# The mixer's last projection as seven block products, with weight sums made in DRAM and ten modulation sums moved

## The chip, the core and the metric

The kernel runs on one core of a Trainium2 chip, in one launch. The metric is the device time of that core in microseconds (us). TensorE multiplies, VectorE (DVE) and ScalarE (ACT) do elementwise work, GpSimd (POOL) does elementwise work and issues DMAs, and SyncE (SP) issues DMAs.

## What is computed

One block with 1024 positions and 1024 channels, all float32:

```python
h = rms_norm(x, norm_mix_g) * (1 + sc1) + sh1
proj = h @ w_in                                  # 7168 columns
y_a = (b * causal_dwconv3(c * v)) @ w_short_out
u = causal_dwconv31(v2 * sigmoid(gl)) + bias
y_b = silu(layer_norm(u)) @ w_conf_out
mix = (g_a * y_a + g_b * y_b) @ w_o              # the projection that changes
x = x + g1 * mix
h2 = rms_norm(x, norm_ffn_g) * (1 + sc2) + sh2
a, bgate = split(h2 @ w_ffn_in, 2)
x = x + g2 * ((silu(a) * bgate) @ w_ffn_out)
out = rms_norm(x, final_norm_g)
```

`sh1, sc1, g1, sh2, sc2, g2` are six modulation vectors, `silu(c) @ w_ada + b_ada`, of 1024 each.

## The kernel before

Activations lie transposed, 128 channels on the partitions and the 1024 positions in two halves `h` of 512 columns. Every operand is held as a high part `h` in fp32r and a remainder `l`, and a product of a 128x128 weight block with a 128x512 operand is three matmuls, high by high, low by high and high by low (`mm3`, L505, L506, L508). Weights come by `load` (SP, L228) into the `raw` buffers, ScalarE casts the high part `wh` (L244), and VectorE or GpSimd subtracts to get `wl` (L245). `fetch` keeps `AHEAD` = 2 weights in front of the one in use.

Most projections run in duals: two output blocks of 128 rows at a time, as a Strassen-like scheme with seven products, `"1265734"` (`PRODUCTS`). `product` is one of them: 2 x 4 x 3 = 24 matmuls of 512 columns. "1" and "2" take plain weight blocks, "4" too, and "5", "6", "7" and "3" take sums of weight blocks, as well as sums of operand blocks. The stages on the profile are: the first norm (to 65 us), the projection of the inputs, 12 duals `w_duals` (65 to 561; from dual 3 on the remainders are GpSimd's), the short convolution's projection `ya` (to 635), the conformer's `yb` (to 711), the last one `mix` (to 799), the feed-forward part's first projection, 11 duals (to 1222), its second (to 1411), and the last norm.

In `mix`, alone among them, no seven products are used: `col_block` makes 8 blocks of output rows in each of the two halves, each from 8 weight blocks, 2 x 8 x 8 x 3 = 384 matmuls. Its evacuation (L1471, VectorE) is x + g1 times the result, with x reloaded as `xr` (GpSimd's queue, L1466); the new x goes to `x1_dram` (L1474) and its square (ScalarE, L1475) into one running sum per half (VectorE, L1481). The sum of the first half is taken over the partitions by TensorE inside `mix` (`norm_2_first`), the second's in the first product of the feed-forward part. Ten modulation sums (numbers 30 to 39 in `ADA_ORDER`) are made there too: `load_b` loads 512 KB from `ada`, and VectorE multiplies and adds in one instruction (`modulation_of`, L486).

The weight sums of `yb` are made in SBUF (`conf_units`): six accumulating DMAs on GpSimd's queue (L398) and two additions on VectorE. Gates `gb` are loaded on that queue too (L1431), and half of the merged results `ma` are summed there by accumulating DMAs (L1403). The first two duals of the feed-forward part make their weight sums by VectorE (`dual_units`). A wait of one engine's instruction holds all that stand behind it on that engine; a scheduler sets the order of each engine from the program and from `issue_after`, and TensorE's order may interleave two products.

## Time and profile before

| | us |
|---|---|
| median of 3 runs | 1442.96 (1442.72 to 1443.38) |
| the profiled execution | 1443.7 |
| its span | 1441.9 |
| TensorE busy | 1428.6 (99%), 6322 matmuls |
| VectorE busy | 1198.8 (83%) |
| ScalarE busy | 655.2 (45%) |
| GpSimd busy | 522.0 (36%) |

The granted clock was 0.998. A row of a group names the line, the engine, the operation and what it writes and reads (`out<-in`), then the shape and the count. A row of waits gives who waited for whom, us in total, how often, and the longest. A row of the table by stage gives the stretch in us from the span's start, its length, the busy time and instructions of each engine, TensorE's granted clock, the busy share of the 16 DMA engines (the sum of the packets' time, so it can pass 1) and the GB/s moved. A row of a DMA queue gives packets, MB and the share of 16 engines; a row of DMA issues the count, the KB of one, and the median us from issue to landing.

### The profile page before, as it was taken

Reading aid. Unit: us, or ns where it says so; the run is one execution under the profiler, and the core shown is the slowest. Engines: PE = TensorE matmul, PEld = TensorE weight load, DVE = VectorE, ACT = ScalarE, POOL = GpSimd, SP = SyncE. Lnnn points to the kernel's source line nnn. Section 1 sums busy time; section 2 is a strip of 40 time slices with the busy share of each in tenths; the row PEclk is TensorE's granted clock in tenths of the full one; section 3 lists DMA queues with packets and bytes.
Section 4 is the critical chain, followed back from the end, with each engine's and each line's share of the span. In section 5 each row is a group of like instructions: output and inputs, shape, how many; then the busy total and the mean of one; then the engine's idle time right before and its main releaser. Section 6 shows DMA issues by size and latency. Waiting matters only on the chain.

```text
span 1441.9 us, 17770 instructions
## 1 busy us (share of the span) xinstructions
PE 1428.6 (99%) x6322; PEld 1173.5 (81%) x6322; DVE 1198.8 (83%) x1665; ACT 655.2 (45%) x963; POOL 522.0 (36%) x512
## 2 busy tenths in 40 slices
PE   8999999999999999999999999999999999999997
PEld 4888888888888888888888888888888888888887
DVE  7996999999899999989988898877777665866676
ACT  4873333333343457567426474533444443321235
POOL 0017777777677562013311001110111015563405
PEclk9999999999999999999999999999999999999999
DMA  9743233333335578768886248645555449996903
GB/s 349 282 162 90 72 117 117 103 117 103 132 124 183 161 244 296 219 193 203 223 317 228 79 141 267 205 149 186 185 175 161 138 143 358 389 372 191 340 0 117
DMA packets 95946, 275.04 MB, mean 191 GB/s; under 512 B 10945, under 2 KB 12993, under 8 KB 95858
## 3 DMA queue, kind: packets, MB, share of 16 engines
q1 hardware_dynamic: 46672, 148.92, 30.6%
q0 software_dynamic: 44000, 111.36, 25.6%
q10 hardware_dynamic: 5186, 13.64, 2.5%
q8 instruction: 49, 0.80, 0.2%
q14 instruction: 39, 0.32, 0.1%
HBM read 203.09 MB, written 67.63 MB: 188 GB/s over the span
## 4 chain that ended last, share of the span: by engine, by line
PE 97%; POOL 1%; DVE 0%; issue 0%; POOLq 0%
PE bank L506 14%; PE bank L505 14%; PE bank L508 14%; PE x L508 8%; PE x L506 8%; PE x L505 8%; PE z L506 4%; PE z L508 4%; PE z L505 4%; PE y L508 3%; PE y L506 3%; PE y L505 3%; PE mix L506 2%; PE mix L508 2%; PE mix L505 2%; PE lead L501 1%
## 5 line engine op out<-in xcount | busy, mean ns | idle before, releaser
L244 ACT CAST wh<-raw 128x1024 fp32r<-128x1024 f32 (+2 forms) x254 | 263.0, 1037 | 394.7 <-PE bank L506 138.1
L245 DVE TENSOR_TENSOR wl<-raw,wh 128x1024 fp32r<-128x1024 f32 (+2 forms) x176 | 212.4, 1208 | 38.1 <-ACT wh L244 35.5
L245 POOL TENSOR_TENSOR wl<-raw,wh 128x1024 fp32r<-128x1024 f32 x78 | 194.4, 2500 | 91.1 <-ACT wh L244 90.1
L1168 DVE SCALAR_TENSOR_TENSOR c<-diff,vec,c 128x512 f32<-128x512 f32 x232 | 163.4, 749 | 1.5
L1644 POOL DMA_DIRECT2D hid<-stage x70 | 37.4, 535 | 343.3 <-DVE stage L554 326.8
L505 PE MATMUL bank<-th,wh 128*128 128x512 f32 x336 | 130.7, 389 | 0.0
L506 PE MATMUL bank<-tl,wh 128*128 128x512 f32 x336 | 130.7, 389 | 0.0
L508 PE MATMUL bank<-th,wl 128*128 128x512 f32 x336 | 130.7, 389 | 0.0
L505 PEld LDWEIGHTS bank<-th,wh 128*128 128x128 f32 x336 | 63.1, 188 | 13.2
L508 PEld LDWEIGHTS bank<-th,wl 128*128 128x128 f32 x336 | 63.1, 188 | 13.1
L506 PEld LDWEIGHTS bank<-tl,wh 128*128 128x128 f32 x336 | 63.1, 188 | 13.0
L553 ACT CAST stage<-g 128x512 fp32r<-128x512 f32 x60 | 37.3, 622 | 74.7 <-DMA hid<-stage 41.0
L506 PE MATMUL x<-tl,wh 128*128 128x512 f32 x176 | 68.5, 389 | 0.0
L505 PE MATMUL x<-th,wh 128*128 128x512 f32 x176 | 68.5, 389 | 0.0
L508 PE MATMUL x<-th,wl 128*128 128x512 f32 x176 | 68.4, 390 | 0.0
L1168 DVE SCALAR_TENSOR_TENSOR c<-u,wsum,c 128x512 f32<-128x512 f32 x96 | 66.8, 750 | 0.8
L554 DVE TENSOR_TENSOR stage<-g,stage 128x512 fp32r<-128x512 f32 x60 | 41.2, 688 | 27.9 <-ACT stage L553 27.7
L1668 POOL DMA_DIRECT2D th<-hid x77 | 41.1, 534 | 52.2 <-PE x L508 26.4
L1668 POOL DMA_DIRECT2D tl<-hid x77 | 41.2, 535 | 19.6 <-DMA tl<-hid 5.6
L265 DVE TENSOR_TENSOR raw<-raw 128x1024 f32<-128x1024 f32 (+1 forms) x15 | 17.8, 1188 | 36.4 <-DMA raw<-in_w_fi 24.1
L486 DVE CUSTOM_DVE_ANT_0 raw<-raw,cs,vec 128x1024 f32<-128x1024 f32 x24 | 39.1, 1639 | 9.5 <-DMA raw<-in_ada 5.4
L505 PE MATMUL bank<-t2h,wh 128*128 128x512 f32 x112 | 43.6, 389 | 0.0
(833 smaller groups left out, 4143.1 us busy)
## 6 DMA issues: line engine op xcount, KB each, us to landing
hid<-stage POOLq DMA_DIRECT2D x70, 512.0 KB, 4.8
raw<-in_w_duals SPq DMA_DIRECT2D x65, 512.0 KB, 3.6
raw<-in_w_fi SPq DMA_DIRECT2D x54, 512.0 KB, 4.3
th<-hid POOLq DMA_DIRECT2D x77, 256.0 KB, 6.0
tl<-hid POOLq DMA_DIRECT2D x77, 256.0 KB, 6.0
ada<-in_ada SPq DMA_DIRECT2D x24, 512.0 KB, 5.9
raw<-in_ada SPq DMA_DIRECT2D x24, 512.0 KB, 4.7
raw<-in_w_fo SPq DMA_DIRECT2D x16, 512.0 KB, 6.1
```

The lines of the kernel that those rows point to most:

```text
L244: hi = nc.scalar.copy(wh, raw)
L245: lo = lo_engine.tensor_tensor(wl, raw, f32(wh), ALU.subtract)
L265: eng.tensor_tensor(a["s1"], a["21"], a["22"], ALU.add)
L486: nc.vector.tensor_tensor_reduce(out=raw, in0=raw, in1=cs, scale=1.0, scalar=col(V_ADA, b), op0=ALU.mult, op1=ALU.add, accum_out=modc(b),)
L505: nc.tensor.matmul(ps, wh, xh, start=first, stop=False, skip_group_check=again)
L506: nc.tensor.matmul(ps, wh, xl, start=False, stop=False, skip_group_check=again)
L508: mm3.ins = nc.tensor.matmul(ps, wl, xh, start=False, stop=last, skip_group_check=again).ins
L553: t_split.act = nc.scalar.copy(hi, src).ins
L554: t_split.ins = nc.vector.tensor_tensor(lo, src, f32(hi), ALU.subtract).ins
L1168: tap.ins = nc.vector.scalar_tensor_tensor(out=out, in0=src[:, s : s + H], scalar=wt, in1=acc, op0=ALU.mult, op1=ALU.add).ins
L1644: nc.gpsimd.dma_start(hid_dram[key], s)
L1668: nc.gpsimd.dma_start(t, hid_dram[key][:, s])
```

## The change

- `mix` becomes two duals of seven products, in the order `"1267453"` (`MIX_ORDER`), 336 matmuls. The sums of operand blocks are made by VectorE (`m_6`) and by eight accumulating DMAs of GpSimd's queue (`onto`, L592 of the kernel after); "7" and "4" take negated splits. The squares' running sums are partly added by `onto` too, three one after another for each half.
- Of the three stages `yb`, `mix` and the first two duals of the feed-forward part, the sums of weight blocks are made in DRAM (`Summed`): 24 copies of 512 KB on SP's queue (L395) and 24 accumulating DMAs on GpSimd's (L399), one of each per product from the first of the input projection on, an accumulate at least three products behind its copy. These stages then load the sums like plain weights; `conf_units` and the early sums go.
- Of the ten modulation sums five (30 to 34) are made in the input projection, one in each of duals 5 to 9, a multiplication on GpSimd and a sum by ScalarE, and five (35 to 39) on VectorE beside `ya`.
- In the feed-forward part, the second half's norm is begun one product later, and eight differences of VectorE become accumulating DMAs.

```diff
+NORM_2_AT = (1, "5")
+NORM_2_ROWS = {(1, "5"): (0, 1, 2, 3), (0, "3"): (4, 5), (1, "3"): (6, 7)}
...
-CONF_ORDER = [(d, m) for m in "1256" for d in range(2)] + [(0, "3")] + [(d, m) for m in "74" for d in range(2)] + [(1, "3")]
+CONF_ORDER = [(d, m) for m in "1256" for d in range(2)] + [(0, "3"), (0, "7"), (0, "4"), (1, "7"), (1, "4"), (1, "3")]
+MIX_ORDER = [(d, m) for m in "1267453" for d in range(2)]
...
+SUMS_FROM, SUM_LAG, PITCH = 0, 3, 16
+
+
+MOD_APART, N_APART, APART_AT, APART_FROM = 30, 5, "6", 5
...
-    def conf_units(mats, d):
...
-        def add(raw, b):
-            conf_adds.append(nc.gpsimd.dma_start(raw, mat[b], accum_op=ALU.add).ins)
-            return raw
-
-        def unit(m):
-            if m == "5":
-                raw = a["s1"] = add(get("22"), "21")
-            elif m == "6":
-                lo = split_w.lo
-                raw = a["s2"] = get("11", (rawp, rawbp)[d])
-                with tc.issue_after(lo):
-                    nc.vector.tensor_tensor(raw, raw, a["s1"], ALU.add)
-            elif m == "7":
-                raw = add(get("21"), "11")
-            elif m == "3":
-                raw = add(a["s2"], "12")
-            else:
-                raw = get({"1": "11", "2": "12", "4": "22"}[m])
-            return split_w(raw, 1024, () if m in "12" else (split.act, split.ins))
-
+    class Summed:
+
+
+        def __init__(self, name, mats):
+            self.a = dict(zip(("11", "12", "21", "22"), mats))
+            self.s = {m: dram.tile([P, T + PITCH], F32, name=f"{name}_{m}")[:, :T] for m in "6573"}
+
+        def copy(self, m):
+            nc.sync.dma_start(self.s[m], self.a[{"5": "22", "7": "11", "6": "11", "3": "12"}[m]])
+
+        def add(self, m):
+            src = {"5": self.a["21"], "7": self.a["21"], "6": self.s["5"], "3": self.s["6"]}[m]
+            nc.gpsimd.dma_start(self.s[m], src, accum_op=ALU.add)
+
+        def unit(self, m, after=()):
+            src = self.s[m] if m in self.s else self.a[{"1": "11", "2": "12", "4": "22"}[m]]
+            return split_w(load(src), 1024, after)
+
+    summed = {(n, d): Summed(f"{n}{d}", [w[d, m] for m in range(4)])
+              for n, w in (("yb", w_conf), ("mix", w_o), ("in", w_fi)) for d in range(2)}
+    to_copy = [(u, m) for u in summed.values() for m in "5763"]
+    to_add, sum_at = list(to_copy), {}
+
+    def sums_step(n):
+
+        if to_copy:
+            u, m = to_copy.pop(0)
+            u.copy(m)
+            sum_at[u, m] = n
+        for u, m in to_add[:4]:
+            parts_at = sum_at.get((u, m), n), *(sum_at.get((u, q, "sum"), n) for q in {"6": "5", "3": "6"}.get(m, ""))
+            if max(parts_at) <= n - SUM_LAG:
+                u.add(m)
+                sum_at[u, m, "sum"] = n
+                to_add.remove((u, m))
+                return
+
+    def units_of(n, d, after=None):
+        return {m: (lambda m=m: summed[n, d].unit(m, (split.act, split.ins) if after and m not in after else ())) for m in PRODUCTS}
...
-    yb_units = [conf_units([w_conf[d, m] for m in range(4)], d) for d in range(2)]
+    yb_units = [units_of("yb", d, "12") for d in range(2)]
     plan += [yb_units[d][m] for d, m in yb_order]
-    plan += [(w_o[k], 1024) for ks in (range(KC), SECOND[KEPT:]) for k in ks]
+    mix_w = [units_of("mix", d, "-") for d in range(2)]
+    plan += [mix_w[d][m] for d, m in MIX_ORDER]
...
+    def modulation_apart(i, raw):
+
+        b = ADA_ORDER[i]
+        nc.gpsimd.tensor_tensor(raw, raw, cs, ALU.mult)
+        yield
+        nc.scalar.activation(raw, raw, AF.Copy, accum_out=modc(b))
+        yield
...
+        if negative:
+            split.act = nc.scalar.activation(hi, src, AF.Copy, scale=-1.0).ins
+            split.ins = minus(lo, src, f32(hi))
+        else:
+            split.act = nc.scalar.copy(hi, src).ins
+            split.ins = nc.vector.tensor_tensor(lo, src, f32(hi), ALU.subtract).ins
...
+    def onto(a, b):
+
+        return nc.gpsimd.dma_start(a, b, accum_op=ALU.add).ins
...
+        if d >= SUMS_FROM:
+            with tc.issue_after(load.ins), tc.issue_after(split_w.lo):
+                sums_step(win_order.index((d, m)))
...
+        if begun_mods:
+            with tc.issue_after(split_w.hi):
+                next(begun_mods.pop())
+        if m == APART_AT and d >= APART_FROM and apart:
+            begun_mods.append(modulation_apart(apart[0], load(ada[apart.pop(0)], home=dual_units.home)))
+            with tc.issue_after(split_w.lo):
+                next(begun_mods[0])
...
+    later, whole = list(range(MOD_APART + N_APART, 40)), []
+
+    def late_modulation(step, behind):
+
+        if step % 2 == 0:
+            if whole:
+                with tc.issue_after(behind):
+                    modulation_of(*whole.pop())
+        elif later:
+            whole.append((later.pop(0), diffp.tile([P, T + CK - 1], F32, tag="diff", name="ada")[:, :T]))
+            with tc.issue_after(load.ins):
+                nc.sync.dma_start(whole[0][1], ada[whole[0][0]])
...
-    def mix(i, h):
-        j = SECOND[i] if h else i
-        xr = g_tile("xr")
-        nc.gpsimd.dma_start(xr, xT[j, :, halves[h]])
-        (o,) = col_block((second_w if h else first_w)(i), mg, (h,), "mix", SECOND if h else [*range(0, KC, 2), *range(1, KC, 2)])
...
+    sums, xrs = {}, {}
+
+    def xr_loads(d, m):
+        row, h = {"2": (0, 0), "6": (0, 1), "7": (1, 1), "4": (1, 0)}.get(m, (0, None))
+        for i in range(2 * (h is not None)):
+            j = 4 * d + 2 * i + row
+            xrs[j, h] = g_tile("xr")
+            nc.gpsimd.dma_start(xrs[j, h], xT[j, :, halves[h]])
+
+    def x1_done(j, h, sq, ins):
         dst = x1[j][:, halves[h]]
-        evac = nc.vector.scalar_tensor_tensor(out=dst, in0=o, scalar=modc(16 + j), in1=xr, op0=ALU.mult, op1=ALU.add)
-        if (i, h) == (KC - 1, 0):
-            mix.half_0 = evac.ins
         nc.gpsimd.dma_start(x1_dram[j][:, halves[h]], dst)
-        sq = nc.scalar.activation(xr, dst, AF.Square, scale=1.0 / 32.0)
-        if (i, h) == (KC - 1, 1):
-            load_rsqrt(sq.ins)
-        if i == 0:
-            sums[h] = xr
+        mix.sq = nc.scalar.activation(sq, dst, AF.Square, scale=1.0 / 32.0).ins
+        if h not in sums:
+            sums[h] = sq
+        elif j % 2 == h:
+            mix.add = onto(sums[h], sq)
+        elif h:
+            with tc.issue_after(h2_of.lo):
+                mix.add = nc.vector.tensor_tensor(sums[h], sums[h], sq, ALU.add).ins
         else:
-            mix.add = nc.vector.tensor_tensor(sums[h], sums[h], xr, ALU.add).ins
+            mix.add = nc.vector.tensor_tensor(sums[h], sums[h], sq, ALU.add).ins
+        mix.half_0 = ins
+
+    def mix_evac(d, banks):
+
+        def evac(i, m, ps):
+            if m == "1":
+                nc.scalar.copy(banks["y", i], ps)
+                return
+            row, h = {"2": (0, 0), "6": (0, 1), "3": (0, 1), "7": (1, 1), "5": (1, 1), "4": (1, 0)}[m]
+            j = 4 * d + 2 * i + row
+            if x1[j] is None:
+                x1[j] = ucp.tile([P, T + CK - 1], F32, tag="uc", name=f"x1{j}")[:, :T]
+            dst = x1[j][:, halves[h]]
+            src = dst if m in "53" else xrs.pop((j, h))
+            ins = nc.vector.scalar_tensor_tensor(
+                out=dst, in0=ps, scalar=ngm[:, j : j + 1] if row else modc(16 + j), in1=src, op0=ALU.mult, op1=ALU.add
+            ).ins
+            if m in "24":
+                x1_done(j, h, src, ins)
+            elif m in "53":
+                x1_done(j, h, g_tile("sq"), ins)
...
+        def m_6(k):
+            nc.vector.tensor_tensor(b[0, 1][k], b[0, 0][k], b[0, 1][k], ALU.subtract)
+            t2m[k] = hl_tile("t2m", F32)
+            minus(t2m[k], b[0, 1][k], b[1, 1][k])
+            for r in range(2):
+                onto(b[r, 0][k], t2m[k])
+            tm_split("6", k, t2m[k])
+
+        def m_7(k):
+            tm_split("7", k, b[0, 0][k], True)
+
+        def m_4(k):
+            tm_split("4", k, b[1, 0][k], True)
+
+        steps = {
+            (0, "2"): each(m_6, 0, 1), (1, "2"): each(m_6, 2, 3), (0, "6"): each(m_7, *range(KH)),
+            (1, "6"): each(m_4, *range(KH)), (0, "7"): lambda: [tm_split("5", k, b[0, 1][k]) for k in range(KH)],
+            (0, "4"): lambda: [tm_split("3", k, b[1, 1][k]) for k in range(KH)],
+        }
+        for d, m in MIX_ORDER:
+            xr_loads(d, m)
+            if (d, m) == NORM_2_AT:
+                norm_2_first()
+            product(banks[d], m, tm[m], evacs[d], onto="2")
+            if (d, m) in NORM_2_ROWS:
+                norm_2_rows(NORM_2_ROWS[d, m])
+            if (d, m) == MIX_ORDER[-1]:
+                load_rsqrt(mix.sq)
+            steps.get((d, m), lambda: None)()
+            yield d, m
...
-        nc.vector.tensor_tensor(b11, b11, b12, ALU.subtract)
+        norm_2_half.scaled.append(h2_of.scaled)
+        nc.vector.tensor_tensor(b12, b11, b12, ALU.subtract)
         t2.append(hl_tile("t2", dt=F32))
-        minus(t2[k], b11, b22)
+        minus(t2[k], b12, b22)
+        for i in (k, k + KH):
+            onto(x1[i][:, halves[0]], t2[k])
         ts["6"][k] = t_pair("t2")
         t_split(t2[k], *ts["6"][k])
...
             for k in range(KH):
-                if m == "4":
-                    with tc.issue_after(los[k - 2]) if k > 1 else ExitStack():
-                        minus(b21[k], t2[k], b21[k])
                 ts[m][k] = t_pair("t" + m)
-                t_split({"5": x1[k][:, halves[0]], "7": b12[k], "3": b22[k], "4": b21[k]}[m], *ts[m][k])
-                los.append(t_split.ins)
+                row, h = {"5": (k, 1), "7": (k, 0), "3": (k + KH, 1), "4": (k + KH, 0)}[m]
+                t_split(x1[row][:, halves[h]], *ts[m][k], negative=m in "74")
...
-    in_units = [dual_units([w_fi[d, m] for m in range(4)], 1024, EARLY[d]) for d in range(N_IN)]
+    in_units = [units_of("in", d, "-") if d < 2 else dual_units([w_fi[d, m] for m in range(4)], 1024, EARLY[d]) for d in range(N_IN)]
...
-    sums = {}
-    for h in range(2):
-        for i in range(KC):
-            mix(i, h)
-            if h == 0:
-                mg_split(i, 1)
-                for b in [32 + i] + [MOD_FROM + n_mod + i] * (MOD_FROM + n_mod + i < 32):
-                    load_b(b)
...
-                    affine(aff2, k, 32, vec, V_GFFN)
-                norm_2_first()
...
-    in_order = [(0, "1"), (0, "2"), (1, "1"), (1, "2"), (2, "1")] + [(d, m) for d in range(2) for m in PRODUCTS[2:]]
+    in_order = [(0, "1"), (1, "1"), (0, "2"), (2, "1"), (1, "2")] + [(d, m) for d in range(2) for m in PRODUCTS[2:]]
...
+    ngm = cp.tile([P, KC], F32, name="ngm")
+    nc.vector.tensor_scalar(ngm, mod[:, 16:24], -1.0, None, ALU.mult)
...
-    in_product(0, "1", norm_2_start)
+    in_product(0, "1")
+    in_product(1, "1", norm_2_start)
+    for t, k in shift_2:
+        with tc.issue_after(r2[4]):
+            nc.scalar.activation(t, t, AF.Identity, bias=modc(24 + k))
...
-        "w_o": _cols(i["w_o"][0], j),
+        "w_o": _duals(i["w_o"][0], [j[::2], j[1::2]], [range(KC // 2), range(KC // 2, KC)]),
```

In the input projection, SP's queue held before nothing but loads. `raw` is a weight's buffer, `in_w_duals` the weights, `in_ada` the modulation's.

```order
L228 DMA raw<-in_w_first 128x896
L228 DMA raw<-in_w_plain 128x1024
L228 DMA raw<-in_w_duals 128x1024 x25
L228 DMA raw<-in_ada 128x1024 x2
L228 DMA raw<-in_w_duals 128x1024 x4
```

Now a copy into a sum (`yb_7` is the sum for product "7" of `yb`, and so on) stands between most loads, on SP.

```order
L236 DMA raw<-in_w_duals 128x1024
L395 DMA yb_7_116<-in_w_conf 128x1024
L236 DMA raw<-in_w_duals 128x1024
L395 DMA yb_5_115<-in_w_conf 128x1024
L236 DMA raw<-in_w_duals 128x1024
L395 DMA yb_6_114<-in_w_conf 128x1024
L395 DMA yb_3_117<-in_w_conf 128x1024
```

On GpSimd, at the same place, weight remainders (`wl`) stood behind one another and behind weight sums for the input projection itself:

```order
L324 TENSOR_TENSOR raw<-raw 128x1024 x2
L245 TENSOR_TENSOR wl<-raw,wh 128x1024 x2
L324 TENSOR_TENSOR raw<-raw 128x1024 x2
L245 TENSOR_TENSOR wl<-raw,wh 128x1024 x5
L265 TENSOR_TENSOR raw<-raw 128x1024
```

Now an accumulating DMA stands between them, and it waits for the copy and for the sums that it reads:

```order
L399 DMA yb_6_114<-yb_5_115 128x1024
L253 TENSOR_TENSOR wl<-raw,wh 128x1024
L399 DMA mix_5_119<-in_w_o 128x1024
L253 TENSOR_TENSOR wl<-raw,wh 128x1024
L399 DMA mix_7_120<-in_w_o 128x1024
L253 TENSOR_TENSOR wl<-raw,wh 128x1024
L399 DMA yb_3_117<-yb_6_114 128x1024
```

In `mix`, GpSimd's queue held reloads of x (`xr`), the last gate accumulates (`ma`), and stores of the new x:

```order
L1466 DMA xr_6100<-in_xT 128x512
L1403 DMA ma41_5192<-gb_5909 128x512
L1403 DMA ma61_5207<-gb_5911 128x512
L1466 DMA xr_6145<-in_xT 128x512
L1474 DMA x1_dram0_5949<-x10_5994 128x512
L1466 DMA xr_6190<-in_xT 128x512
```

Now the three accumulates onto the first half's sum (`xr_6141` holds it) stand among them, and the reloads of x for the next products behind these; `xr_6318` is that for the second block of the second dual's "6":

```order
L592 DMA xr_6141<-xr_6143 128x512
L1519 DMA x1_dram4_6056<-x14_6224 128x512
L1515 DMA xr_6316<-in_xT 128x512
L592 DMA xr_6141<-xr_6202 128x512
L1519 DMA x1_dram6_6058<-x16_6241 128x512
L592 DMA xr_6141<-xr_6204 128x512
L1515 DMA xr_6318<-in_xT 128x512
L1515 DMA xr_6368<-in_xT 128x512
```

A load that stood behind one store stands behind two waits now. The second half's sum has such a chain of three as well (onto `sq_6579`), and the matmul that takes it over the partitions stands on TensorE in the second product of the feed-forward part.

167 lines of the change are left out of this document (83 added, 84 removed).

## The prediction

> **What bounds the kernel now.** I read the busy shares of the page first, then the waits of TensorE, then its timeline inside the last projection of the mixer.
>
> ```profile
> PE 1428.6 (99%) x6322; PEld 1173.5 (81%) x6322; DVE 1198.8 (83%) x1665; ACT 655.2 (45%) x963; POOL 522.0 (36%) x512
> ...
> PE clock L721 <- ACT sq L668: 1.9, 1, 1.9
> PE clock L721 <- DVE ones_r L739: 1.6, 1, 1.6
> PE clock L721 <- DVE newton L780: 0.7, 1, 0.7
> ...
> 723.72 0.39 PE L506 MATMUL mix<-mg40l,wh 128*128 128x512 f32 x1
> ...
> 725.31 0.39 PE L508 MATMUL mix<-mg10h,wl 128*128 128x512 f32 x1
> ```
>
> TensorE is busy 99% of the span, and its only three waits are for the clock's warm-up matmuls at the start, before any product. In the projection the eighth matmul starts 1.59 us after the first, 1.59/7 = 0.227 us each, though each shows 0.39 us (they overlap). So TensorE issues without a gap, and the time is its matmul count times 0.227 us. A change pays by what it takes from that count, as long as everything that feeds TensorE stays in time.
>
> The second view is the table by stage: projection of the inputs (to 561), the short convolution's projection (561 to 638), the conformer's (to 714), the last projection (to 802), the start of the feed-forward part, and a late stretch.
>
> ```profile
> core 0: us, PE busy (x) PEld busy (x) DVE busy (x) ACT busy (x) POOL busy (x), PEclk, DMA share, GB/s
> ...
> 95.00:240.00 145.00, 145.00 (x642) 120.05 (x641) 123.62 (x179) 60.66 (x87) 99.03 (x50) 1.00 0.33 107
> 240.00:480.00 240.00, 240.00 (x1061) 198.72 (x1060) 229.04 (x336) 87.97 (x120) 174.51 (x85) 1.00 0.37 123
> ...
> 561.00:638.00 77.00, 77.00 (x337) 62.60 (x336) 67.38 (x98) 45.22 (x67) 7.22 (x9) 1.00 0.77 222
> ...
> 714.00:758.00 44.00, 44.00 (x196) 36.44 (x195) 35.40 (x60) 14.09 (x21) 9.45 (x17) 1.00 0.86 308
> 758.00:802.00 44.00, 44.00 (x195) 36.22 (x194) 35.13 (x46) 24.96 (x37) 8.12 (x15) 1.00 0.62 209
> ...
> 1225.00:1260.00 35.00, 35.00 (x156) 28.96 (x156) 29.50 (x41) 12.46 (x18) 20.47 (x39) 1.00 1.18 389
> ```
>
> TensorE fills every row. VectorE is the next engine: idle 11.0 us of 240 in the middle of the input projection, 9.6 us of 77 beside the short convolution's projection, 17.5 us of 88 in the last one.
>
> **The change, part by part.**
>
> *Seven products instead of eight.* The last projection was 16 column blocks x 8 x 3 = 384 matmuls. It becomes 2 duals x 7 products x 24 = 336. All other matmuls stay (6242 rows in the order before, 6194 after). 48 x 0.227 = 10.9 us, all on the path: **-10.9 us**.
>
> *VectorE's work in that stretch.* The prices are these:
>
> ```profile
> L486 DVE CUSTOM_DVE_ANT_0 raw<-raw,cs,vec x24: 1249/1283/3420, 191.0 to 744.8; 128x1024 f32<-128x1024 f32 x24
> ...
> 788.11 0.75 DVE L1471 SCALAR_TENSOR_TENSOR x<-mix,mod,xr 128x512 f32<-128x512 f32 x1 [2.04 <-PE mix L508]
> 788.97 1.23 DVE L245 TENSOR_TENSOR wl<-raw,wh 128x1024 fp32r<-128x1024 f32 x1
> 790.11 0.68 DVE L1481 TENSOR_TENSOR xr<-xr 128x512 f32<-128x512 f32 x1
> ...
> DVE x L1471 <- PE mix L508: 12.3, 6, 3.2
> ```
>
> Removed: ten modulation sums (10 x 1.28 = 12.8), six of fourteen additions of squares (6 x 0.68 = 4.1). Added: 28 splits for 16 (12 x 0.68 = 8.2), eight differences (5.4), 24 evacuations for 16 (8 x 0.75 = 6.0), one more weight remainder (1.2). Net +3.9 us, or less, since neighbours overlap by some 0.08 us. VectorE had 35.40 + 35.13 = 70.5 us in 88; it now has about 74 in 88 - 10.9 = 77. Its cover falls from 17.5 to some 3 us. In the old stretch 12.3 us of its idleness was waiting for TensorE's next result, so it had been ahead. Work may lag past the end of the stretch into the feed-forward part's first four products, where eight differences and four weight sums leave VectorE. I cost it at nothing; if the cover is gone, the first thing late is the second half's norm (below).
>
> *Accumulating DMAs in place of VectorE's additions.* They stand in GpSimd's queue, and everything behind one that waits, waits. The nearest rows are the gate accumulates of the conformer's projection and the reloads of x, both 256 KB:
>
> ```profile
> L1403 POOL DMA_DIRECT2D ma<-gb x12: 860/896/1259, 653.6 to 717.4; - x12
> DMA to landing us min/median/max: 3.2/6.1/8.2
> ...
> L1466 POOL DMA_DIRECT2D xr<-in_xT x16: 538/538/570, 712.5 to 780.4; - x16
> DMA to landing us min/median/max: 2.9/5.3/6.1
> ```
>
> Two places have a deadline. With the products laid out at 5.44 us each from 711.2 (no stall), the second dual's "2" ends at 733.1.
> (a) Three squares are added one on another into the first half's sum. The first is issued at about 731, the next when it has landed, the third when that has; only behind the third stands the load of x for the second dual's "6". At 6.1 us each the third is issued by 744, and the x lands 5.3 us later, at 750; it is needed at about 752, when "7" starts in that bank. At 8.2 and 6.1 it lands at 755: 3 us late.
> (b) The second half's sum: three serial accumulates from about 773, ended at 773 + 3x. The matmul that sums them stands at 796.1 and can bear an end up to about 787, x = 4.7 us. At 3.2 us there is no stall, at 6.1 it is 4.3 us, at 8.2 it is 10.6 us.
> The twelve measured ones ran beside six 512 KB accumulates; these run where the ten modulation blocks are gone from the queues, so I take x between 3.2 and 6.1, 4.8 us: **+0.5 us** for (a) and (b) together, ends 0 and 10.6.
> The fit in the Trainium skill ("DMA: Bandwidth & Descriptors", the section on the anatomy of one DMA) gives a DMA from GpSimd 2.0 us plus its bytes over 436 GB/s, as an estimate 2.6 us here. By it the term would be 0; the measured median is more than twice that, with the queues full, and I go by the row.
>
> *Weight sums in DRAM.* 24 copies of 512 KB enter SP's queue and 24 accumulates GpSimd's between about 95 and 240 us, one of each per product. Nothing in the trace copies DRAM to DRAM, so the nearest are an accumulate from DRAM to SBUF, alone in an 11 us window, with the plain traffic beside it, and the landings with queues nearly idle (from 95 to 240) and full (from 1225 to 1260):
>
> ```profile
> q0 software_dynamic: 144, 0.52, 28.5%
> q1 hardware_dynamic: 152, 0.56, 16.1%
> ...
> raw<-in_w_duals SPq DMA_DIRECT2D x21, 512.0 KB, 3.6
> ...
> raw<-in_w_fo SPq DMA_DIRECT2D x3, 512.0 KB, 7.2
> ...
> ACT wh L244 <- PE bank L506: 107.8, 47, 4.4
> ```
>
> 0.285 x 11 = 3.1 us of all 16 engines per accumulate, 0.161 x 11 x 0.52/0.56 = 1.7 us per plain 512 KB. 24 x 4.8 = 115 us on top of 0.33 x 145 = 48: a share of 163/145 = 1.12. The late stretch ran at 1.18 and TensorE did not stop. There loads landed in 7.2 us instead of 3.6. The casts of 95 to 480 wait for TensorE to give a buffer back (47 times, 107.8 us) and never for a load, so 4 us more are hidden: **0**. GpSimd issues for 24 x 0.9 = 21.5 us more and was idle 46 us in that stretch; SP's loads wait behind 24 more issues, within the same 4 us.
>
> *Modulation sums moved.* Five go to GpSimd in the later duals of the projection, five to VectorE beside the short convolution's projection: 5 x 1.28 = 6.4 us into 9.6 us of idleness there, **0**, though the variance matmul behind it has little left. For the five on GpSimd:
>
> ```profile
> L313 POOL TENSOR_TENSOR raw<-raw 128x1024 f32<-128x1024 f32 x7 | 16.9, 2413 | 0.5
> ...
> L432 DVE TENSOR_TENSOR raw<-raw x4: 1215/1221/1226, 431.9 to 510.1; 128x1024 f32<-128x1024 f32 x4
> ...
> L433 DVE TENSOR_TENSOR raw<-raw x4: 3030/3049/3252, 433.7 to 511.9; 128x1024 f32<-128x1024 f32 x4
> ```
>
> 2.41 us each of GpSimd, which has 65 us of 240 free. The same VectorE addition took 1.22 us at L432 and 3.05 at L433, which started while GpSimd ran a like one: each of the five may hold VectorE for 1.8 us, 9 us of the 11.0 us it has free from 240 to 480. Ends 0 and 9 less that cover: **0**.
> The page "SBUF — State Buffer" of the Trainium skill (on the shared port pair) calls this an exclusive lock, the loser blocked for the whole instruction; L433 agrees, and this rule speaks against the change, since it makes the 9 us the likely figure rather than the bound.
>
> *Conformer's projection.* Six 512 KB accumulates and two VectorE additions (2 x 1.22) go, plain loads come: relief where the weights stand closest to their use. **0**, since TensorE did not wait there.
>
> Sum: -10.9 + 0.5 = -10.4 us. The profiled execution took 1443.7 us (span 1441.9 and 1.8 around it), 0.7 over the runs' median of 1442.96. 1443.7 - 10.4 = 1433.3, and against the median **1432.6 us**.
>
> **The rivals.**
> *A serial accumulate or a thin cover is late in the last projection.* For it: the median of 6.1 us, and VectorE's 3 us of cover. At 6.1 us, 1442.96 - 10.9 + 4.3 = 1436.4; at 8.2, 1442.7, no gain. Against: fewer bytes in these queues than beside the twelve.
> *VectorE falls behind, in the later duals (9 us against 11.0 free) or beside the short convolution's projection (6.4 against 9.6).* Against it: convolution work, most of what VectorE does there, is due only at the stage's end. A miss of 2 to 5 us: 1434 to 1437.
> *The sums starve the weights (the slow side).* An accumulate whose both ends are DRAM may cost more than 3.1 us. Per product of 5.44 us the engines must serve an accumulate y, a copy 1.7 and 21/145 x 5.44 = 0.8 weight loads of 1.7 us. Above y = 2.4 us a backlog grows by y - 2.4 per product; it may reach some 16 us, three products, before GpSimd blocks on a copy or a partial sum that has not landed, with the weight remainders behind it. At 3.1 us the 24 leave 17 us, at the edge. To lose 10.9 + 2.9 us beyond that, 24(y - 2.4) - 16 = 13.8, y = 3.6 us. At 4.8 it costs 41.6 us: 1474. Against it: the share is a sum over packets that overlap (1.18 is above one), and 389 GB/s were moved at that share, while these 145 us moved 107 and now need 24 x 1.05 MB more, 107 + 25.2/0.145 = 281 GB/s.
> The Trainium skill ("DMA: Bandwidth & Descriptors", the specifications) puts the HBM limit of one core at 358 GB/s; counting reads and writes, two for a copy and three for an accumulate, 63 + 15 MB would as an estimate take 219 us where there are 145, which is this rival by another way. The late stretch's 389 GB/s is above that limit, but no run here shows it for such copies.
>
> **How the numbers follow.** Forecast as summed: 0.62, 1431.5 to 1434. Late accumulate 0.14 (0.02 of it no gain), VectorE behind 0.08 (0.01 no gain), starved weights 0.16 (0.04 within, 0.12 slower). A change under 0.2%, 2.9 us, can't be told from none. Faster 0.62 + 0.12 + 0.07 = 0.81, same 0.07, slower 0.12. The range 1431.5 to 1440 leaves out the starved weights and the worst of the accumulates, under 0.2.
>
> **What the profile after would show.** Right: 48 fewer matmuls, TensorE's waits still only at the start, the last projection 77 us long, the DMA share from 95 to 240 near 1 with casts waiting for TensorE and not for loads, the accumulates at 4 to 5 us. Wrong: a wait of TensorE on the matmul of the sum near 796, or in the "7" products near 752 (rival one); waits on a weight cast or remainder between 95 and 300 (the slow side); convolution steps bunched at the end of the projection (rival two).

## The result, and the profile after

The changed kernel is slower: 1465.45 us median (1464.17 to 1466.35, 4 runs) against 1442.84 us before (1442.39 to 1443.38), a ratio of 1.0156, 95% interval [1.0138, 1.0174]. The forecast was 1432.6 and the range ended at 1440.0. The profiled execution took 1466.35 us, its span is 1464.6.

The page's busy line and TensorE's waits of the changed kernel (who waited for whom; us, times, longest):

```profile
PE 1431.0 (98%) x6274; PEld 1168.0 (80%) x6274; DVE 1209.5 (83%) x1661; ACT 669.2 (46%) x990; POOL 571.0 (39%) x557
...
PE bank L527 <- DVE x L1544: 5.5, 2, 3.6
PE bank L527 <- DVE bank L885: 3.1, 1, 3.1
PE bank L530 <- POOL wl L253: 2.9, 2, 1.5
PE bank L527 <- ACT bank L1536: 2.8, 1, 2.8
PE bank L527 <- ACT bank L941: 1.7, 2, 0.8
...
PE bank L528 <- DVE tl L584: 1.5, 1, 1.5
PE ss L713 <- DVE sq L1527: 1.0, 1, 1.0
```

The 48 matmuls are gone (6322 to 6274), 10.9 us as forecast, but TensorE, which had waited for nothing after its warm-up, now waits for VectorE, GpSimd and ScalarE in many places. The table by stage, first before, then after, tells where. A stretch that TensorE fills holds 1/0.227 matmuls per us.

```profile
65.00:561.00 496.00, 496.00 (x2190) 410.72 (x2189) 460.36 (x661) 216.79 (x314) 321.39 (x162) 1.00 0.43 141
```

```profile
65.00:561.00 496.00, 484.96 (x2111) 396.86 (x2111) 461.12 (x640) 206.43 (x300) 352.67 (x189) 0.99 0.62 186
...
654.00:730.00 76.00, 76.00 (x337) 62.72 (x336) 72.75 (x108) 47.16 (x72) 16.84 (x25) 1.00 0.67 186
730.00:819.00 89.00, 80.72 (x340) 65.27 (x339) 60.87 (x83) 41.99 (x63) 31.48 (x47) 0.96 0.81 220
```

In the input projection 79 matmuls fewer were started in the same 496 us: 79 x 0.227 = 17.9 us lost. The last projection took 89 us where 14 products are 77. What a matmul's start lies behind its predecessor's beyond 0.227 us is time lost; added up over the matmuls of a stage it gives the loss by stage: 17.7 us in the input projection, 4.1 in the short convolution's (1.6 before), 0.1 in the conformer's, 12.4 in the last, 2.7 in the start of the feed-forward part (0.8 before): 37.0 against 2.8, which less 10.9 is the 22.6 us between the medians, within 1 us. These losses by stage are used for all runs below. Each is read from one execution, and kernels with the same source in a stage differ in it: the input projection's loss was 17.7, 17.5 and 18.9 us in three such kernels, but 8.9 and 5.8, or 7.7, 15.7 and 9.8, or 40.4 and 30.1 in others. A difference of a few us between two runs there shows nothing by itself.

**In the input projection** TensorE's direct waits up to 300 us are 5.8 us, 5.0 of them for VectorE and none for a weight; behind that they are 5.2, 2.9 of them for weight remainders of GpSimd (`wl`). On VectorE one group stands out, the fourteen multiply-and-add instructions of the modulation (one line, one form, before and after; busy us, mean ns):

```profile
L486 DVE CUSTOM_DVE_ANT_0 raw<-raw,cs,vec 128x1024 f32<-128x1024 f32 x14 | 26.4, 1894 | 9.5 <-DMA raw<-in_ada 5.4 <-issue 4.0
```

```profile
L508 DVE CUSTOM_DVE_ANT_0 raw<-raw,cs,vec 128x1024 f32<-128x1024 f32 x14 | 44.5, 3180 | 11.1 <-DMA raw<-in_ada 8.5 <-issue 2.6
```

The same fourteen instructions took 18 us more. The timeline of the longest, VectorE's row first, then GpSimd's of the same moment (start, duration, us):

```profile
195.21 9.54 DVE L508 CUSTOM_DVE_ANT_0 raw<-raw,cs,vec 128x1024 f32<-128x1024 f32 x1 [2.29 <-DMA raw<-in_ada]
...
194.45 1.09 POOL L399 DMA_DIRECT2D mix<-mix  x1
195.01 2.95 POOL L253 TENSOR_TENSOR wl<-raw,wh 128x1024 fp32r<-128x1024 f32 x1
197.35 1.38 POOL L399 DMA_DIRECT2D in<-in_w_fi  x1
197.92 3.38 POOL L1217 TENSOR_TENSOR tot<-tot,u 128x512 f32<-128x512 f32 x2
200.43 3.22 POOL L253 TENSOR_TENSOR wl<-raw,wh 128x1024 fp32r<-128x1024 f32 x1
202.77 1.65 POOL L399 DMA_DIRECT2D in<-in_w_fi  x1
203.62 3.39 POOL L253 TENSOR_TENSOR wl<-raw,wh 128x1024 fp32r<-128x1024 f32 x1
```

A 1.28 us instruction stood 9.54 us, beside two remainders, two additions and the start of a third remainder. Each of GpSimd's rows begins before the one ahead has ended, and the accumulating issues leave no gap between its elementwise instructions. If the held instruction worked in its last 1.28 us, it began at 203.47, about where the second of these remainders ends (203.65). Before, the longest such instruction took 3.42 us, no more than one GpSimd instruction of 2.4 us beside its own time. The next evacuations of banks stood behind it on VectorE, and TensorE stopped: two of its starts, at 213.1 and 216.6, lie 3.48 us apart.

**In the last projection** the chain of waits runs through GpSimd's queue:

```profile
732.20 3.77 DMA ma<-gb
...
738.14 6.12 DMA ma<-gb
...
753.09 10.03 DMA ma<-t2m
...
775.23 5.16 DMA xr<-in_xT
```

The reloads of x wait at the head of the queue until a gate's accumulate has landed and given its buffer free; the accumulates onto `ma41` and `ma61` stand behind them and landed at 744.3 and 750.1, where the plan without stalls needed them by 730. The operand differences `t2m` wait for those, eight accumulates onto the operands follow one another (5.8 to 10.4 us to land), and behind these the chain of sums and the load of x for "6".

### The profile page after: what moved, and what is told of

Read it like the earlier page. It is cut to its first block, busy times and chain, and to the rows that moved or that the text cites. A ratio compares the mean times of both kernels' runs of the same rounds, so it can differ in the third digit from the quotient of the medians.

```text
span 1464.6 us, 17821 instructions
## 1 busy us (share of the span) xinstructions
PE 1431.0 (98%) x6274; PEld 1168.0 (80%) x6274; DVE 1209.5 (83%) x1661; ACT 669.2 (46%) x990; POOL 571.0 (39%) x557
## 4 chain that ended last, share of the span: by engine, by line
PE 45%; DVE 8%; DMA 5%; issue 4%; POOL 3%; ACT 2%; POOLq 0%; ACTq 0%; DVEq 0%
PE x L528 8%; PE x L530 8%; PE x L527 8%; PE z L527 4%; PE z L530 4%; PE z L528 4%; PE y L530 2%; PE y L527 2%; PE y L528 2%; DMA raw<-in_w_short 1%; PE bank L530 1%; PE bank L527 1%; PE bank L528 1%; DVE c L1186 1%; DMA ma<-gb 1%
## 5 line engine op out<-in xcount | busy, mean ns | idle before, releaser
L253 DVE TENSOR_TENSOR wl<-raw,wh 128x1024 fp32r<-128x1024 f32 (+2 forms) x178 | 215.5, 1211 | 49.1 <-ACT wh L252 47.0
L253 POOL TENSOR_TENSOR wl<-raw,wh 128x1024 fp32r<-128x1024 f32 x78 | 202.9, 2616 | 75.3 <-ACT wh L252 69.0
L508 DVE CUSTOM_DVE_ANT_0 raw<-raw,cs,vec 128x1024 f32<-128x1024 f32 x14 | 44.5, 3180 | 11.1 <-DMA raw<-in_ada 8.5
L1779 POOL DMA_DIRECT2D tl<-hid x77 | 41.0, 533 | 21.5 <-DMA tl<-hid 6.5
L530 PE MATMUL bank<-t2h,wl 128*128 128x512 f32 x112 | 44.1, 393 | 1.5 <-POOL wl L253 1.4
```

Of the source, the lines that this page charges most:

```text
L253: lo = lo_engine.tensor_tensor(wl, raw, f32(wh), ALU.subtract)
L508: nc.vector.tensor_tensor_reduce(out=raw, in0=raw, in1=cs, scale=1.0, scalar=col(V_ADA, b), op0=ALU.mult, op1=ALU.add, accum_out=modc(b),)
L530: mm3.ins = nc.tensor.matmul(ps, wl, xh, start=False, stop=last, skip_group_check=again).ins
L1779: nc.gpsimd.dma_start(t, hid_dram[key][:, s])
```

## The experiments

Each was one run with a profile beside a run of the kernel before (1442.3 to 1443.8 us), except three that are given with their intervals. Line numbers in the text are the changed kernel's; the rows of a run have its own, which can be a few higher.

**Without the sums.** `sums_step` is not called and the products load plain blocks.

> The 24 copies and 24 accumulating DMAs of the input projection are left out; the products that would load a sum load one plain block of the same size. Theory (GpSimd's fuller queue holds VectorE's additions with two SBUF inputs, and VectorE's lateness stops TensorE): the 14 multiply-and-add instructions of VectorE in the projection go back from 44.5 us together to 26 to 32, and of the 17.6 us that TensorE lost between 65 and 561 us some 11 to 14 come back: 1452 to 1455. Rival (the DMA engines are short and weights come late): the same time here, this run alone does not part the two. Rival (the five GpSimd multiplications of the later duals): the loss after 240 us stays and only some 8 us come back, 1457.

1455.92 us, 9.5 less: loss in the input projection 8.9 instead of 17.7, the fourteen instructions 30.4 us. So about half of the loss there goes with the sums. The rest is there without them. The five modulation sums moved to GpSimd are one candidate, but no run leaves out both.

**The DMA load without GpSimd.**

```diff
-            nc.sync.dma_start(self.s[m], self.a[{"5": "22", ...}[m]])
+            for dst in (self.s[m], *self.more[m]):
+                nc.sync.dma_start(dst, self.a[{"5": "22", ...}[m]])
-                u.add(m)
```

> Each of the 24 accumulating DMAs of GpSimd's queue is replaced by two more plain copies on SP's queue into other buffers, so the sums are not formed; the DMA engines have 24 x 3 x 1.7 = 122 us of such work instead of 115, GpSimd has none of it. Theory (GpSimd's queue and its hold on VectorE): the projection loses no more than without the sums, 1452 to 1456, and the multiply-and-add instructions take 26 to 32 us. Rival (DMA engines short): the loss of 17 us stays, 1463 or later, with waits on weights.

1463.05 us. Both had a part: the fourteen instructions fell to 27.1 us, as the theory wanted, but the loss was 16.0 us, as the rival wanted, with waits on weights and operands instead of on held banks:

```profile
L509 DVE CUSTOM_DVE_ANT_0 raw<-raw,cs,vec 128x1024 f32<-128x1024 f32 x14 | 27.1, 1943 | 10.8 <-DMA raw<-in_ada 7.3 <-issue 3.6
...
PE bank L529 <- DVE tl L585: 3.0, 1, 3.0
PE bank L531 <- POOL wl L253: 3.0, 1, 3.0
...
PE bank L528 <- ACT wh L252: 1.6, 1, 1.6
```

Copies on the loads' own queue, 122 us of them by the estimate, go with late weights, and the fourteen are no longer held. So a loss of nearly the same size came about without the hold, and this run does not say what the hold costs.

**The held instructions taken out.**

```diff
-                    modulation_of(MOD_FROM + n_mod, load(ada[MOD_FROM + n_mod], home=dual_units.home))
+                    load(ada[MOD_FROM + n_mod], home=dual_units.home)
+                    nc.vector.memset(modc(ADA_ORDER[MOD_FROM + n_mod]), 0.5)
```

> The 14 multiply-and-add instructions of VectorE in the input projection are replaced by a memset of their one-column result; their loads stay, and so do all copies and accumulates. Theory (these instructions are where GpSimd's full queue holds VectorE): 44.5 us of VectorE's time go, and the stalls at 213, 250 and 300 to 460 us with them, at least 12 of 17.6 us: 1451 to 1454; the first stall, at 121 us, stays. Rival (DMA engines short): DMA traffic is the same, so the loss stays within 3 us of what it is, 1462 to 1465.

1450.36 us, 15.1 less, with every copy and accumulate still there: the loss in the projection fell to 6.6 us. The rival's 1462 is out. The run also takes away the 26.4 us that these instructions took before the change, so it shows that VectorE's lateness was on the path, not that all of it was the hold.

**Plain DMAs in the accumulates' places.** `accum_op=ALU.add` is left out at L399.

> The 24 accumulating DMAs stay in their places in GpSimd's queue, with their waits, but copy instead of adding, so the sums are wrong in value and the DMA engines have less to do (24 x 1.7 instead of 24 x 3.1 us). Theory (VectorE's multiply-and-add waits until GpSimd's run of instructions ends, and a DMA issue between them closes the gap): the 14 instructions stay at 38 us or more together, and at least two thirds of the loss from 200 to 480 us stays: 1460 to 1466. Rival (it is the adding that loads GpSimd or the DMA engines): they fall to 26 to 31 us, as without the sums, and 8 to 10 us come back: 1455 to 1457.

1457.79 us, between the two: the fourteen 33.1 us, the loss 8.0, which is that of the run without the sums. The same place as above, with the same instructions in GpSimd's queue:

```profile
196.29 3.08 DVE L508 CUSTOM_DVE_ANT_0 raw<-raw,cs,vec 128x1024 f32<-128x1024 f32 x1 [2.92 <-DMA raw<-in_ada]
...
195.42 2.40 POOL L253 TENSOR_TENSOR wl<-raw,wh 128x1024 fp32r<-128x1024 f32 x1
197.76 0.54 POOL L399 DMA_DIRECT2D in<-in_w_fi  x1
198.31 4.44 POOL L1217 TENSOR_TENSOR tot<-tot,u 128x512 f32<-128x512 f32 x2
```

A GpSimd issue without the addition took 0.54 us in place of 0.74 to 1.65. The elementwise instructions around it lie 0.49 us apart (197.82 to 198.31) where they touched before, and VectorE's instruction got in there: 3.08 us in place of 9.54, and no hold above 3.43. So it isn't that any DMA issue on GpSimd closes the gap: those of accumulating DMAs do. The DMA engines had less to do here as well, so the run does not part the two for the loss.

**Ten sums late.** `N_APART = 0`.

> The five GpSimd multiplications of the later duals go; their five modulation sums join the other five on VectorE beside the short convolution's and the conformer's projections. Theory (GpSimd's queue holds VectorE): the loss of TensorE between 300 and 480 us, 6.9 us, shrinks to 1 to 3, and the stage from 561 to 714 us gains 0 to 3 us of loss from 6.4 us more VectorE work: 1459 to 1463. Rival (that loss comes from what was late before, not from the multiplications): the loss between 300 and 480 stays within 2 us, 1465 to 1468.

1470.52 us, worse than both bounds. From 300 to 480 us the loss did shrink, from 6.9 to 3.4, but with VectorE's five more instructions 4.4 us were lost in the conformer's projection and 5 more in the last (17.4), whose operands come from there.

**The sums spaced.** One step at every third product.

> The same 24 copies and 24 accumulates, but one of each at every third product instead of every product, so they run to about 450 us instead of 260. Theory (a GpSimd queue without a gap holds VectorE, and short DMA engines delay the first loads): the stalls at 121 and 213 to 250 us go, the 14 multiply-and-add instructions take 30 to 36 us together, and half or more of the 17.6 us of the projection comes back: 1453 to 1458. Rival (GpSimd has too little free time in any place beside the five multiplications): the loss only moves later, 1462 to 1466.

1485.64 us, 20 more; both numbers of the expectation were wrong. The DMA share from 95 to 240 us fell from 0.83 to 0.50, yet the projection lost 36.3 us, and the fourteen took 52.4 (the longest 10.53): all duals with modulation sums now had accumulates beside them. From 240 to 480 us TensorE has 954 matmuls where the changed kernel had 1020 (its rows first, then this run's):

```profile
95.00:240.00 145.00, 140.39 (x604) 114.84 (x603) 125.00 (x167) 55.98 (x80) 106.96 (x64) 0.98 0.83 234
240.00:480.00 240.00, 233.57 (x1020) 190.41 (x1020) 230.00 (x327) 90.36 (x128) 189.80 (x94) 1.00 0.45 143
...
95.00:240.00 145.00, 143.06 (x623) 117.71 (x622) 126.23 (x169) 57.50 (x82) 102.38 (x56) 0.99 0.50 151
240.00:480.00 240.00, 224.46 (x954) 182.15 (x953) 227.12 (x312) 84.80 (x120) 178.34 (x97) 0.97 0.60 177
...
ACT wh L252 <- DMA raw<-in_w_duals: 29.7, 5, 10.7
```

From 240 us on the casts also waited 29.7 us for loads (7.3 in the changed kernel). A late VectorE that gives buffers back late would do that, but it is not shown. The loss went where the accumulates went: 3.8 us instead of 8.1 from 95 to 240 us, 23.7 instead of 8.8 from there to 480. The share of the DMA engines alone is not what decides, since 0.60 of them went with more loss than 0.83.

**The feed-forward sums deferred; the multiplications moved.** First the eight accumulates for the feed-forward part wait for dual 10, then also `APART_AT = "3"`.

> The eight accumulates for the feed-forward part wait until dual 10, after the last of VectorE's modulation sums in the projection; the other sixteen run as before, to about 207 us. Theory (VectorE held by GpSimd): the sums at 195 us are still held by the last of the sixteen, those from 240 us on are not held by an accumulate; the 14 take 34 to 39 us together, and 3 to 6 us of the loss come back: 1459 to 1462. Rival (spread elsewhere, they do the same harm there): 1465 or later.

> As the run with the eight accumulates late, and the five GpSimd multiplications stand at product 3 of their duals instead of 6, where VectorE has no modulation sum. Theory: the sums of duals 5 to 9 go from 22.2 us of ten (before and in this kernel alike some 1.3 to 3.5 each) to 15 to 19, and of the 6.9 us lost between 300 and 480 us some 2 to 5 come back: 1455 to 1460. Rival (GpSimd's 2.4 us each make the weights' remainders late in any place): no change against that run.

1467.26 and 1492.41 us: the theories missed both. In the first the fourteen fell to 38.2 us, as the theory wanted, but the loss stayed (18.0: some 6 us up to 240, nearly all the rest from 380 us on), as the rival said. So less hold did not bring less loss. In the second the fourteen took 38.2 us as well, and the loss rose to 40.4. One reason that I had not seen: ScalarE's sum of the product (L500) waits for GpSimd's multiplication, and the evacuations behind it on ScalarE with it.

```profile
ACT raw L501 <- POOL raw L499: 29.5, 5, 7.6
```

(4.0 us in the first of the two.) TensorE's waits there are mostly on ScalarE's and VectorE's evacuations, up to 4.5 us.

**The last projection.** The reloads of x on SP's queue (`nc.sync` for `nc.gpsimd` in `xr_loads`), then on another run all 14 accumulating DMAs as VectorE additions.

> In the last projection the 16 reloads of x go from GpSimd's queue to SP's; all else as in the changed kernel. Theory (the reloads wait for buffers at the head of GpSimd's queue, and the last gate accumulates and the sums stand behind them): the accumulates onto ma41 and ma61, which landed at 744.3 and 750.1, land 6 to 10 us earlier, and of the 12.4 us that TensorE lost from 740 to 790 us 6 to 10 come back: 1455 to 1459. Rival (the accumulates are slow in themselves, 8 to 10 us in a row of eight, or VectorE's cover of 3 us is too thin): the loss stays within 3 us, 1462 to 1465.

> In the last projection all 14 accumulating DMAs (eight onto the operands, six onto the sums of squares) become VectorE additions of 128x512; the reloads of x stay on GpSimd's queue. Theory (the accumulates' landings, 5 to 10 us, and their places in GpSimd's queue set the end there): the sum matmul near 827 waits no more, and TensorE's loss from 740 to 840 us, some 15 us, falls by 4 to 8: 1457 to 1461. Rival (VectorE's cover of 3 us): 14 x 0.6 = 8.4 us more VectorE work in that stretch make it the wait, and the loss stays or grows, 1465 to 1470.

1460.61 and 1462.24 us. With the reloads away `ma41` landed at 739.4 instead of 744.3, and the loss there went from 12.4 to 5.5. With the additions on VectorE it went to 9.4, and the wait at the sum matmul to nothing (loss 1.0 after 2.7). Both moved the wait the way their theories said, but the times lie between theory and rival; neither alone took it away, and in the first 1.4 us more were lost in the feed-forward part.

**All moves together**, the second with the sums of the kernel with both deferrals:

> Together: the sums spaced to every third product, all ten modulation sums on VectorE beside the two middle projections, the reloads of x and of the conformer's gates on SP's queue instead of GpSimd's, and the sums of squares added by VectorE. If the losses are separate, of 33 us some 12 to 15 come back in the projection, 8 to 10 in the last projection and 2 at the sum matmul: 1440 to 1445, against 1442.8 before. Rival (VectorE is the bound from 500 us on and takes back what is freed): 1448 to 1455.

> As the run before it, with the reloads of x and the gates' loads of the conformer's projection on SP's queue, the sums of squares on VectorE, and four of the eight accumulates onto the operands of the last projection on VectorE. If the losses are separate: 6 to 9 us back from 740 to 840 us: 1447 to 1452. Rival (VectorE's 3 us of cover): the stall moves to the splits that VectorE makes there, and less than 3 us come back, 1453 to 1458.

1463.24 and 1467.85 us, both above theory and rival. In the first the loss in the last projection was 6.0, but the spaced sums lost 20.5 in the input projection and the ten late ones 4.4 after it. In the second the last projection lost nothing:

```profile
746.00:823.00 77.00, 77.00 (x341) 63.73 (x340) 67.70 (x94) 42.38 (x63) 12.77 (x20) 1.00 0.69 213
```

77 us, as planned, with ten more additions on VectorE, which is still 9.3 us idle. The input projection lost 30.1 us in that kernel, so the time shows none of it.

**The bound without sums, and the sums by stage.** The last projection as in the run before; first without sums, then with all of them, then also with ten late.

> The 24 copies and accumulates are left out (products load plain blocks instead of sums), and the last projection has the reloads of x and the gates on SP's queue, the sums of squares and four of the eight operand accumulates on VectorE. If the losses of the two places are separate, the 10.5 us that the run without the sums still lost from 740 to 790 us go from its 1455.9: 1444 to 1448. If freeing one place makes the other later, 1450 or more.

> All sums are formed, with the last projection as in the run before: the copies at every second product; the eight accumulates for the conformer's projection in the first duals, before VectorE's first modulation sum of the projection, those for the last projection beside the short convolution's, those for the feed-forward part beside the conformer's, where GpSimd has little elementwise work. Theory (an accumulate costs only where it stands beside a VectorE instruction with two SBUF inputs): the 14 instructions take 28 to 34 us, the projection loses no more than without sums, 1445 to 1450. Rival (an accumulate costs wherever it stands, by DMA engines or queue): 1455 or later, with waits on weights in the two middle projections.

> As the run before, and the five GpSimd multiplications of the later duals go; all ten modulation sums are on VectorE beside the two middle projections. The loss from 300 to 480 us falls to some 3 us; the two middle projections lose 4 to 6 us, as in the earlier run with ten late. Theory (losses separate): 1443 to 1449. Rival (VectorE is then late at the start of the last projection): 1450 or later.

1441.46, 1449.55 and 1459.89 us. The losses are separate: without sums the 10.9 us of the last projection go, and the rest is 5.8 + 5.0 + 1.0 (input projection, short convolution's, feed-forward). That kernel leaves the sums out, and yet is 1.4 to 2.4 us under the runs of before, no clear difference in one run. The second is the fastest that forms the sums, 8.1 us behind the first. Its time lies in the expected range by luck: its accumulates had not gone where I put them. The scheduler issued those of the later stages from 166 to 345 us, and the projection lost 17.5 us, not the 5.8 of the run without sums. The fourteen took only 30.5 us there. TensorE now waited mostly for remainders that GpSimd made late, and GpSimd, at the head of its queue, for the copies that its accumulates read:

```profile
PE bank L531 <- POOL wl L253: 8.9, 7, 2.3
...
POOL mix L399 <- DMA mix<-in_w_o: 19.4, 3, 9.7
```

In the third, without the five GpSimd multiplications, the projection lost 21.4 us, some 11 of them from 300 to 480 us where 3 were expected: taking these multiplications away did not help there.

**The accumulates tied to their places**, the first for the last projection ahead of the short convolution's own, the second with those for the feed-forward part in the last projection, the third with those for the last projection behind the short convolution's own.

> In the run with the sums by stage the scheduler still put accumulates for the later stages between 166 and 310 us, beside the modulation sums. Here they are tied: one copy per product, the eight accumulates for the conformer's projection as in the changed kernel, to about 165 us; those for the last projection in GpSimd's order behind the last remainder of the input projection; those for the feed-forward part between the gate accumulates of the conformer's projection. The last projection is as in the two runs before. Theory (an accumulate costs where it stands beside VectorE's two-input instructions): no accumulate stands between 195 and 555 us, the 14 take 26 to 31 us, and the loss in the projection is at most the 6 us that the run without sums had, plus 2 at 121: 1441 to 1445. Rival (moved to the middle projections they delay the gate accumulates there): a new loss of 3 to 8 us from 640 to 790 us, 1446 to 1450.

> As the run before, but the eight accumulates for the feed-forward part stand behind the stores of the new x in the last projection, from about 750 us, and not beside the gates. Theory: as before in the input projection, and no accumulate stands ahead of a gate accumulate: 1440 to 1444. Rival (they land too late for the sums' loads near 800 us, or delay the stores and the accumulates onto x behind them): a loss at 810 to 850 us, 1445 to 1450.

> As the run with the sums tied, but the eight accumulates for the last projection stand in GpSimd's queue behind the last of the six accumulates that the short convolution's projection needs itself, not ahead of them; those for the feed-forward part stand among and behind the gate accumulates as there. Theory (in that run the 22 us lost from 580 to 640 us came from the accumulates standing ahead of those whose sums TensorE waits for): the loss there falls to the 3 to 4 us of the run without sums, the rest stays: 1440 to 1444, against 1442.9 before. Rival (the bytes, not the order, made the weights late there): a loss of 10 us or more stays, 1450 or later.

| | time, us (4 runs) | ratio, 95% interval | loss: input, short conv., conformer, last, feed-forward |
|---|---|---|---|
| tied | 1462.9 (1461.8 to 1465.4) | 1.0135 [1.0118, 1.0152] | 7.7, 25.1, 0.1, 2.1, 1.1 |
| feed-forward in the last | 1469.5 (1465.1 to 1472.5) | 1.0181 [1.0161, 1.0201] | 15.7, 25.1, 0.1, 1.1, 2.0 |
| behind the last own | 1463.6 (1462.9 to 1466.4) | 1.0146 [1.0129, 1.0162] | 9.8, 10.6, 2.6, 9.7, 1.1 |

The theory held for the input projection in the first: with no accumulate between 165 and 555 us the fourteen took 26.8 us, as before the change, and the loss fell to 7.7. In the other two there is none from 165 to 560 us either, but the fourteen took 32.7 and 32.2 us and the losses were 15.7 and 9.8. So a loss of 8 to 16 us stays without accumulates beside the fourteen, and its cause is open. And the accumulates cost elsewhere. Ahead of the short convolution's own accumulates they made its weights late (a cast waited 11.4 us for one); behind them the loss there fell by 14.5 us, but other loads were slow. Loads of a gate took 7.8 and 10.9 us to land, VectorE waited for them, and the weight remainder behind it let TensorE stand 5.3 us. A load of the modulation took 13.76 us, with the variance of the norm behind it, which cost TensorE 1.1 us:

```profile
625.92 0.69 DVE L895 SCALAR_TENSOR_TENSOR ma<-bank,ga 128x512 f32<-128x512 f32 x1 [2.50 <-DMA ga<-gate_a]
629.67 0.69 DVE L895 SCALAR_TENSOR_TENSOR ma<-bank,ga 128x512 f32<-128x512 f32 x1 [3.06 <-DMA ga<-gate_a]
...
632.76 0.80 PE L533 MATMUL bank<-q7h,wl 128*128 128x512 f32 x1 [5.29 <-DVE wl L253]
...
623.45 13.76 DMA ada<-in_ada
```

The expected 1440 to 1444 did not come, and the rival (the bytes, not the order) fits: 10.6 us of loss there, as it said. Another 9.7 were lost in the last projection, where a weight's cast came 5.2 us late. None of the kernels that form the sums beat the one before.

## Why the prediction was wrong, point by point

- **The removed matmuls: right.** 6274 matmuls, 10.9 us. Without the sums and with the last projection's work on other queues and on VectorE, 1441.46 us had 11.8 us of other losses in it.
- **"Weight sums in DRAM ... 0": the step that failed.** It cost 8 to 9.5 us: the time fell by 9.5 without them, and by 8.1 in the pair with the last projection's moves. I had priced it in the DMA engines, and their share was not more than I had: 0.83 of them from 95 to 240 us where I had 1.12, loads landing in 5.4 us. What I had not priced is GpSimd's queue with 24 accumulating issues in it. I set their 21.5 us against GpSimd's 46 idle ones as if idle time there cost nothing. The runs show two costs of it: VectorE's two-input instructions wait for an opening between GpSimd's (9.54 us with accumulating issues, 3.08 with plain ones in the same places), and where an accumulate waits for its copy, as in the run with the sums by stage, the weight remainders behind it come late. That the first carries most of the 9 us is argued, not shown: the loss was 17.5 and 18.0 us with the fourteen at 30.5 and 38.2.
- **"Modulation sums moved ... 0", with the ends 0 and 9 less the cover: wrong, with the cause in part open.** Without the sums 8.9 us of loss remain in the input projection (5.8 in a like kernel), about the 9 us from which I took off VectorE's cover. No run takes away the five multiplications together with the sums; with the sums in place, taking them away changed the loss from 17.7 to 16.0, and in another kernel from 17.5 to 21.4. The row that I quoted (1.22 against 3.05 us, beside one GpSimd instruction) was right, and I applied it only to the five multiplications, not to the fourteen instructions that were there already beside a queue that I made fuller. The Trainium skill's rule ("SBUF — State Buffer", on the shared port pair: the loser blocked for the whole instruction) agrees with the trace. The 328 convolution steps beside, which read one of their inputs from PSUM, kept 0.75 us in both kernels. The traces add that the hold can last for a whole run of GpSimd instructions, 9.54 us, and not only for one.
- **The accumulates in the last projection: right place, wrong size.** I had +0.5 us; the stage lost 12.4, and 1.9 more were lost behind it. Place (a) stopped TensorE 4.0 us at 777, the load of x for "6" landing at 780.4 behind the chain, as described; at (b) it waited 1.4. But I took the chain to begin in time. It began late, since the reloads of x waited for buffers ahead of the last gate accumulates (moving the reloads away took the loss to 5.5), and the eight accumulates onto the operands (10.4 us at the worst, 8.2 was my bound) I had not costed at all.
- **VectorE's cover of 3 us: not the limit.** Ten more additions on VectorE and no loss in that stage, with 9.3 us of idleness left.
- **The rival on the slow side had a right place and the right sign (0.12 for slower), by another mechanism.** It asked for 3.6 us of the DMA engines per accumulate; the change lost at less, and up to 300 us TensorE waited for no weight. From 95 to 240 us GpSimd's queue moved 9.41 MB, 18 of these 512 KB, in 35.2% of 145 us, 2.8 us each. The 358 GB/s limit of the Trainium skill ("DMA: Bandwidth & Descriptors", the specifications) did not show here. The stretch moved 234 GB/s; with the 20 copies issued in it counted twice, 18 accumulates three times and the rest once, as the prediction counts, that is as an estimate 63 MB in 145 us, some 434 GB/s.

What stays open: what the loss without sums, 5.8 to 15.7 us, is made of, the five multiplications' hold, the wait of ScalarE behind them (5.6 us in the changed kernel) or something else that changed; how the 9 us of the sums divide between the hold and the rest; and why an accumulating issue, but not a plain one, leaves no opening on GpSimd. That a version with the sums in other places would pay isn't excluded; three were tried with the accumulates tied to places, and none did.

## What to carry to other kernels

Before work is put on an idle engine, ask which other engine needs its pauses: here instructions of VectorE with two SBUF inputs got in between GpSimd's, and a fuller GpSimd queue went with a loss of some 9 of the 10.9 us that the removed matmuls gave. A DMA in a queue costs what stands behind it, so follow each one by its buffers and the last thing it waits for. Take each saving apart by stage first: the gain of 10.9 us was real and stood all the time, under losses in four places. And look at a second kernel with the same stage before you price a cause from one loss: 7.7 and 15.7 us came from the same source.

## What the runs showed of the hardware

- An accumulating DMA's issue on GpSimd took about 0.80 us alone and 1.09, 1.38, 1.65 us when the next followed closely, with the instructions around it overlapping; a plain one took 0.54 us.
- After the stalls of 4.0 and 3.2 us in the last projection (at 777 and 749) TensorE ran slower for some 3 us each time: the granted clock of the stage is 0.96, and its matmuls started 0.43 us apart instead of 0.23 (the timeline behind the first; the third row is back at full rate):

```profile
783.07 0.63 PE L527 MATMUL bank<-mg7h,wh 128*128 128x512 f32 x1
783.50 0.63 PE L528 MATMUL bank<-mg7l,wh 128*128 128x512 f32 x1
...
786.22 0.40 PE L530 MATMUL bank<-mg4h,wl 128*128 128x512 f32 x1
```

  Of the 12.4 us lost there some 9.1 are gaps between matmuls, and 3.3 this slower rate. The Trainium skill says this of a TensorE that idled for a window of about 3.4 us ("TensorE: Matmul & The Clock Gate", the part on the clock gate). The traces agree on the slower rate, but here shorter stalls could be enough: 3.2 us in this kernel, 2.6 us at 212 in the run with the feed-forward sums late. One of 3.4 us at 771 in the run without the sums, and the 2.3 us stall at 767 here, show nothing of it. The stall of 4.0 us cost nearly half as much again.
